# Batched 64x64 matmul: b in a block-diagonal tile by cast DMA, a loaded as fp32 in 2 KB runs and cast on VectorE

## The chip, the cores and the metric

The kernel runs on one core of a Trainium2 chip. The metric is the device time of one execution in microseconds; the time before is the median of three runs.

## The reference

```python
"a": np.random.randn(1024, 64, 64).astype(np.float32)
"b": np.random.randn(1024, 64, 64).astype(np.float32)

def reference(a, b):
    return np.matmul(a, b).astype(np.float32)
```

There are 1024 independent products of 64x64 matrices in fp32. Each of a, b and the output holds 4,194,304 numbers, 16.78 MB. Both kernels multiply in bf16 and accumulate in fp32.

## The kernel before

The 1024 matrices are worked off in 16 load groups of 64 (the loop over `lg`). A group has 32 pairs of matrices, and a pair stands on 128 partitions: the rows of the even matrix on partitions 0 to 63, those of the odd one on 64 to 127.

**Loads.** All loads are issued from GpSimd and cast fp32 to bf16 on the way. For a there are two loads a group (L70), one for each half of the partitions; they write only the two diagonal 64x64 blocks of `a_diag` (three buffers in turn, zeroed once by VectorE at L60). For b there are two loads a group (L77), each of 16 pairs. A row of a matrix is 64 numbers: 256 bytes in memory, 128 bytes as bf16.

**Compute.** A group is cut into four compute groups of 8 pairs (the loop over `cg`). TensorE transposes the 8 block-diagonal 128x128 blocks of a (L89), VectorE copies the result out of PSUM (L93), and then TensorE multiplies (L102). Each pair takes two matmuls, with 64 columns of the transposed a as weights, every second one, and the pair's b (64 columns) as the moving operand. The results go to PSUM partitions 0 to 63 or 64 to 127 by turns of two. VectorE copies one half of the results to `o_sb` (L112), ScalarE the other (L113).

**Stores.** Each group ends with one store of 1 MB from SyncE (L121): each partition reads 8 KB of `o_sb` and writes sixteen runs of 512 bytes. SyncE issues nothing else.

**Order.** Each engine works off its instructions in the order in which the tile framework's scheduler has placed them, and an instruction that waits holds up what stands behind it on its engine. Loads run ahead as far as there are buffers: three each of `a_diag`, `b_sb` and `o_sb`.

Of the kernel before, what the change touches and what calls it, by code (L numbers as in the profile page):

```python
# [1 line left out]

# [5 lines left out]

fp32 = mybir.dt.float32  # L10
bf16 = mybir.dt.bfloat16


@with_exitstack
def kernel(
    ctx: ExitStack,
    tc: tile.TileContext,
    a: bass.AP,
    b: bass.AP,
    out: bass.AP,  # L20
):
    nc = tc.nc

    B, M, K = a.shape
    _, _, N = b.shape
    assert (M, K, N) == (64, 64, 64)

    LG = 64 if B % 64 == 0 else B
    CG = 16
    STORE_BF16 = False  # L30
    A_BUFS = 3
    SBUF_BUFS = 3
    PSUM_BUFS = 3

    assert B % LG == 0 and LG % CG == 0
    n_lg = B // LG
    n_cg = LG // CG

    P2_LG = LG // 2
    P2_CG = CG // 2  # L40
    S4_CG = CG // 4

    a_v = a.rearrange("(g p h) r n -> g h r p n", p=P2_LG, h=2)
    b_v = b.rearrange("(g s h) r n -> g h r s n", s=P2_LG, h=2)

    consts = ctx.enter_context(tc.tile_pool(name="consts", bufs=1))
    a_pool = ctx.enter_context(tc.tile_pool(name="a_pool", bufs=1))
    lg_pool = ctx.enter_context(tc.tile_pool(name="lg", bufs=SBUF_BUFS))
    cg_pool = ctx.enter_context(tc.tile_pool(name="cg", bufs=2 * PSUM_BUFS))
    ps_pool = ctx.enter_context(  # L50
        tc.tile_pool(name="ps", bufs=PSUM_BUFS, space=bass.MemoryType.PSUM)
    )

    identity = consts.tile([128, 128], bf16)
    make_identity(nc, identity)

    a_tiles = []
    for ai in range(A_BUFS):
        a_diag = a_pool.tile([128, P2_LG, 128], bf16, name=f"a_diag_{ai}")
        nc.vector.memset(a_diag, 0.0)  # L60
        a_tiles.append(a_diag)

    out_dt = bf16 if STORE_BF16 else fp32

    for lg in range(n_lg):
        i0 = lg * LG

        a_sb = a_tiles[lg % A_BUFS]
        for h in range(2):
            nc.gpsimd.dma_start(  # L70
                out=a_sb[64 * h : 64 * h + 64, :, 64 * h : 64 * h + 64],
                in_=a_v[lg, h],
            )

        b_sb = lg_pool.tile([128, P2_LG, 64], bf16, name="b_sb")
        for s0 in range(0, P2_LG, P2_LG // 2):
            nc.gpsimd.dma_start(  # L77
                out=b_sb[:, s0 : s0 + P2_LG // 2, :],
                in_=b_v[lg, :, :, s0 : s0 + P2_LG // 2, :],
            )  # L80

        o_sb = lg_pool.tile([128, LG // 4, 128], out_dt, name="o_sb")

        for cg in range(n_cg):
            p0 = cg * P2_CG

            t_ps = ps_pool.tile([128, P2_CG, 128], bf16, name="t_ps")
            for pp in range(P2_CG):
                nc.tensor.transpose(  # L89
                    t_ps[:, pp, :], a_sb[:, p0 + pp, :], identity  # L90
                )
            t_sb = cg_pool.tile([128, P2_CG, 128], bf16, name="t_sb")
            nc.vector.tensor_copy(t_sb[:], t_ps[:])  # L93

            o_ps = ps_pool.tile([128, S4_CG, 128], fp32, name="o_ps")
            for pp in range(P2_CG):
                p = p0 + pp
                sigma, colp = pp // 2, pp % 2
                orows = slice(64 * colp, 64 * colp + 64)
                stat = t_sb[:, pp, :].rearrange("k (hh mm) -> k hh mm", hh=2)  # L100
                for j in range(2):
                    nc.tensor.matmul(  # L102
                        o_ps[orows, sigma, 64 * j : 64 * j + 64],
                        stat[:, :, j::2],
                        b_sb[:, p, :],
                        start=True,
                        stop=True,
                    )

            half = S4_CG // 2  # L110
            dst = o_sb[:, cg * S4_CG : (cg + 1) * S4_CG, :]
            nc.vector.tensor_copy(dst[:, :half, :], o_ps[:, :half, :])  # L112
            nc.scalar.copy(dst[:, half:, :], o_ps[:, half:, :])  # L113

        o_dst = out[i0 : i0 + LG].rearrange(
            "(q b4) (t u) c -> b4 t q u c", b4=4, u=2
        )
        if STORE_BF16:
            nc.gpsimd.dma_start(out=o_dst, in_=o_sb[:, :, :])
        else:  # L120
            nc.sync.dma_start(out=o_dst, in_=o_sb[:, :, :])  # L121


# [1 line left out]
_INS = ['a', 'b']  # L125
_OUTS = [((1024, 64, 64), 'float32')]


# [23 lines left out]
```

## Time and profile before

| what | value |
|---|---|
| device time, median of 3 runs | 188.72 us (188.5 to 189.0) |
| span of the profiled execution, first to last instruction | 186.4 us |
| difference, what lies around the span | 2.3 us |
| busy share of TensorE, VectorE, GpSimd, ScalarE | 48%, 40%, 39%, 13% |
| mean granted TensorE clock | 0.656 |
| moved by DMA, counted as it lands | 33.79 MB |
| read from and written to memory | 33.55 MB, 16.78 MB |

The profile shows one execution. A DMA row counts packets and the bytes that land: a load that casts counts its bf16 bytes, half of what it reads. The "share of 16 engines" adds up the times of packets, and packets of one engine can overlap, so it can pass 100%. PEclk and "granted clock" give the TensorE clock as a share of full speed. An engine name with a q (SPq, POOLq) is that engine's issuing queue.

### The profile page before, as it was taken

How to read it: one execution, taken by the hardware profiler on the slowest of the kernel's cores; microseconds unless marked ns; L12 is line 12 of the kernel's file. 1: busy time of each engine (PE TensorE's matmuls, PEld its weight loads, DVE VectorE, ACT ScalarE, POOL GpSimd, SP SyncE). 2: the span in 40 equal slices, each digit the busy share in tenths (PEclk: the TensorE clock that was granted, in tenths of full speed). 3: DMA queues.
4: the chain of work that ended last, by engine and by line, in shares of the span. 5: the costliest groups of instructions: out<-in, count | busy, mean ns of one | idle time of the engine just before them, and what ended most of it. 6: DMA issues, size and time to landing. Idle time of an engine off the chain costs nothing.

```text
span 186.4 us, 3567 instructions
## 1 busy us (share of the span) xinstructions
PE 90.0 (48%) x1536; PEld 75.9 (41%) x1536; DVE 74.6 (40%) x131; ACT 25.1 (13%) x65; POOL 72.4 (39%) x70
## 2 busy tenths in 40 slices
PE   0088126282444814629147480575704867174740
PEld 0077125271334713528036460464503756163630
DVE  6449323344134632426224270353602546044350
ACT  2011301102002110111101120021300113011020
POOL 7998422362424604255132642336322373200000
PEclk9999955559657685585855576555665556755585
DMA  5999999999999999999999999999999999999937
GB/s 36 143 156 157 186 212 213 165 169 215 183 208 157 182 206 186 201 158 194 194 196 192 158 201 186 206 182 157 215 177 212 171 158 204 183 212 177 236 103 205
DMA packets 165136, 33.79 MB, mean 181 GB/s; under 512 B 132352, under 2 KB 165120, under 8 KB 165120
## 3 DMA queue, kind: packets, MB, share of 16 engines
q0 software_dynamic: 132096, 16.78, 140.5%
q1 hardware_dynamic: 33024, 16.78, 42.4%
q8 instruction: 12, 0.20, 0.4%
q14 instruction: 4, 0.03, 0.0%
HBM read 33.55 MB, written 16.78 MB: 270 GB/s over the span
## 4 chain that ended last, share of the span: by engine, by line
DMA 69%; PE 13%; POOL 7%; issue 6%; DVE 2%; ACT 0%; POOLq 0%
DMA b_sb<-in_b_dram 58%; DMA a_diag<-in_a_dram 11%; PE t_ps L89 8%; PE o_ps L102 5%; POOL a_diag L70 4%; POOL b_sb L77 3%; DVE a_diag L60 1%; DVE t_sb L93 0%; DVE o_sb L112 0%; ACT o_sb L113 0%; POOLq L70 0%; POOLq L77 0%
## 5 line engine op out<-in xcount | busy, mean ns | idle before, releaser
L89 PE MATMUL t_ps<-identity,a_diag 128*128 128x128 bf16 x512 | 57.8, 293 | 61.2 <-DMA a_diag<-in_a_dram 61.2
L89 PEld LDWEIGHTS <-a_diag 128*128 128x128 bf16 x512 | 46.4, 134 | 64.4 <-issue 62.4
L93 DVE COPY t_sb<-t_ps 128x1024 bf16<-128x1024 bf16 x64 | 43.6, 691 | 70.6 <-PE t_ps L89 70.3
L77 POOL DMA_DIRECT2D b_sb<-in_b_dram x32 | 37.1, 1164 | 56.3 <-DMA a_diag<-in_a_dram 22.9
L102 PE MATMUL o_ps<-b_sb,t_sb 128*64 128x64 bf16 x1024 | 36.3, 230 | 28.3 <-DMA b_sb<-in_b_dram 24.9
L70 POOL DMA_DIRECT2D a_diag<-in_a_dram x32 | 34.9, 1093 | 31.8 <-DMA b_sb<-in_b_dram 22.5
L102 PEld LDWEIGHTS <-t_sb 128*64 128x64 bf16 x1024 | 29.5, 141 | 39.1 <-issue 19.4
L113 ACT COPY o_sb<-o_ps 128x256 f32<-128x256 f32 x64 | 23.8, 373 | 154.6 <-DVE o_sb L112 154.4
L112 DVE COPY o_sb<-o_ps 128x256 f32<-128x256 f32 x64 | 26.9, 424 | 32.8 <-PE o_ps L102 32.2
L60 DVE MEMSET a_diag<- 128x2048 uint32 x3 | 5.3, 1765 | 2.0 <-PEq L136 1.2
L113 ACT ACT_TABLE_LOAD x1 | 1.3, 1283 | 0.7 <-PEq L136 0.7
masks.py:199 POOL TENSOR_SCALAR_AFFINE_SELECT identity<-identity 128x128 bf16<-128x128 bf16 x1 | 0.3, 307 | 0.1
masks.py:197 POOL MEMSET identity<- 128x128 bf16 x1 | 0.2, 206 | 0.3 <-POOLq L136 0.3
L136 POOL MEMSET const-float32-0.0<- 128x1 f32 x1 | 0.1, 99 | 0.2 <-issue 0.2
L136 POOL MEMSET const-bfloat16-1.0<- 128x1 bf16 x1 | 0.1, 102 | 0.0
L136 POOL MEMSET const-uint8-127<- 128x1 uint8 x1 | 0.1, 102 | 0.0
L136 POOL MEMSET const-float32-1.0<- 128x1 f32 x1 | 0.1, 99 | 0.0
## 6 DMA issues: line engine op xcount, KB each, us to landing
out_dram<-o_sb SPq DMA_DIRECT2D x16, 1024.0 KB, 11.4
b_sb<-in_b_dram POOLq DMA_DIRECT2D x32, 256.0 KB, 19.1
a_diag<-in_a_dram POOLq DMA_DIRECT2D x32, 256.0 KB, 20.3
```

The lines of the kernel that those rows point to most:

```text
L60: nc.vector.memset(a_diag, 0.0)
L70: nc.gpsimd.dma_start(out=a_sb[64 * h : 64 * h + 64, :, 64 * h : 64 * h + 64], in_=a_v[lg, h],)
L77: nc.gpsimd.dma_start(out=b_sb[:, s0 : s0 + P2_LG // 2, :], in_=b_v[lg, :, :, s0 : s0 + P2_LG // 2, :],)
L89: nc.tensor.transpose(t_ps[:, pp, :], a_sb[:, p0 + pp, :], identity)
L93: nc.vector.tensor_copy(t_sb[:], t_ps[:])
L102: nc.tensor.matmul(o_ps[orows, sigma, 64 * j : 64 * j + 64], stat[:, :, j::2], b_sb[:, p, :], start=True, stop=True,)
L112: nc.vector.tensor_copy(dst[:, :half, :], o_ps[:, :half, :])
L113: nc.scalar.copy(dst[:, half:, :], o_ps[:, half:, :])
L136: nc = _bacc.Bacc("TRN2", target_bir_lowering=False, num_devices=1)
```

## The change

The work is still cut into 16 pieces (now called tiles, `t`) of 64 matrices, and the store is written in other words, with the same size and the same runs. The rest is new.

- **b** now makes the block diagonal. A tile of b is `b_bd`, 128 partitions by 16 by 4 by 128, with four buffers that VectorE zeroes at the start. Four matrices share a column of 128 partitions: matrix h stands on partitions 32h to 32h + 31, two rows side by side on each partition. So four loads a tile, each on 32 partitions, still cast from GpSimd, but with runs of 512 bytes in memory and 256 bytes in bf16.
- **a** is loaded as fp32 from SyncE, one load of 1 MB a tile, in runs of 2 KB, three tiles ahead, into four buffers. VectorE then casts it to bf16 and reorders it (`a_bf`).
- **TensorE** makes 16 transposes a tile (half as many as before), each of every second column of `a_bf`. VectorE copies them out of PSUM with a reordering read, four copies of 512 a tile. There are 64 matmuls a tile, as before, but each with 32 columns of weights, 256 columns of b (four blocks of 64) and an output on 32 PSUM partitions, the four strips of 32 in turn; two matmuls accumulate into each result.
- **Output copies** are one per 512 columns, two a tile on ScalarE and two on VectorE.

```diff
-        for h in range(2):
-            nc.gpsimd.dma_start(
-                out=a_sb[64 * h : 64 * h + 64, :, 64 * h : 64 * h + 64],
-                in_=a_v[lg, h],
-            )
...
-        for s0 in range(0, P2_LG, P2_LG // 2):
-            nc.gpsimd.dma_start(
-                out=b_sb[:, s0 : s0 + P2_LG // 2, :],
-                in_=b_v[lg, :, :, s0 : s0 + P2_LG // 2, :],
-            )
...
+    T = 64
+    n_t = B // T
+    AHEAD = 3
+    NB = 4
+    a_v = a.rearrange("(t h g) (mp v) k -> t (g mp) h (v k)", h=4, g=16, v=8)
+    b_v = b.rearrange("(t h g) (kp u) n -> t h kp g (u n)", h=4, g=16, u=2)
+    o_v = out.rearrange("(t hq g4) (mo w) n -> t (g4 mo) hq (w n)", hq=16, g4=4, w=2)
...
+    a_pool = ctx.enter_context(tc.tile_pool(name="a_pool", bufs=NB))
+    at_pool = ctx.enter_context(tc.tile_pool(name="at_pool", bufs=3))
+    o_pool = ctx.enter_context(tc.tile_pool(name="o_pool", bufs=3))
...
+    def load_a(t):
+        a_sb = a_pool.tile([128, 4, 8, 64], fp32, name="a_sb")
+        nc.sync.dma_start(
+            out=a_sb[:].rearrange("p h v k -> p h (v k)"), in_=a_v[t]
+        )
+        a_tiles[t] = a_sb
+    def load_b(t):
+        for h in range(4):
+            nc.gpsimd.dma_start(
+                out=b_tiles[t % NB][32 * h : 32 * h + 32, :, h, :], in_=b_v[t, h]
+            )
+    nc.vector.memset(b_tiles[0][:], 0.0)
+    load_a(0)
+    load_b(0)
+    identity = consts.tile([128, 128], bf16)
+    make_identity(nc, identity)
+    for i in range(1, NB):
+        nc.vector.memset(b_tiles[i][:], 0.0)
+    for t in range(1, AHEAD):
+        load_a(t)
+        load_b(t)
+    for t in range(n_t):
+        if t + AHEAD < n_t:
+            load_a(t + AHEAD)
+            load_b(t + AHEAD)
...
+        nc.vector.tensor_copy(
+            a_bf[:], a_sb[:].rearrange("p h v k -> p v h k")
+        )
+        a_cols = a_bf[:].rearrange("p v h k -> p v (h k)")
...
+                    nc.tensor.transpose(
+                        at_ps[:, vo, u, :], a_cols[:, 2 * vo + w, u::2], identity[:]
+                    )
...
+                nc.vector.tensor_copy(
+                    at_sb[:, w, u, :, :],
+                    at_ps[:, :, u, :].rearrange("p vo q -> p q vo"),
+                )
...
+        for gq in range(4):
+            o_ps = o_psum.tile([128, 2, 4, 64], fp32, name="o_ps")
+            for w in range(2):
+                for u in range(2):
+                    for g4 in range(4):
+                        g = 4 * gq + g4
+                        nc.tensor.matmul(
+                            o_ps[32 * g4 : 32 * g4 + 32, w, :, :],
+                            at_sb[:, w, u, 8 * g : 8 * g + 8, :].rearrange(
+                                "p mp vo -> p (mp vo)"
+                            ),
+                            b_bd[:, g, :, 64 * u : 64 * u + 64],
+                            start=(u == 0),
+                            stop=(u == 1),
+                        )
+            dst = o_sb[:, :, gq, :, :]
+            src = o_ps[:].rearrange("p w h n -> p h w n")
+            if gq % 2 == 0:
+                nc.scalar.copy(dst, src)
+            else:
+                nc.vector.tensor_copy(dst, src)
+        nc.sync.dma_start(
+            out=o_v[t], in_=o_sb[:].rearrange("p h q w n -> p (h q w n)")
+        )
```

More of the change, by code (lines that the diff above doesn't have):

```diff
@@ L25 @@
     _, _, N = b.shape
[L26 to L44, printed above, removed]
-    consts = ctx.enter_context(tc.tile_pool(name="consts", bufs=1))
@@ L47 @@
[L47 to L51, printed above, removed]
-    )
+    assert (M, K, N) == (64, 64, 64) and B % 64 == 0
+    T = 64
[3 more added lines that the diff above has]
+    a_v = a.rearrange("(t h g) (mp v) k -> t (g mp) h (v k)", h=4, g=16, v=8)
@@ new lines @@
+    b_v = b.rearrange("(t h g) (kp u) n -> t h kp g (u n)", h=4, g=16, u=2)
+    o_v = out.rearrange("(t hq g4) (mo w) n -> t (g4 mo) hq (w n)", hq=16, g4=4, w=2)
+    consts = ctx.enter_context(tc.tile_pool(name="consts", bufs=1))
+    a_pool = ctx.enter_context(tc.tile_pool(name="a_pool", bufs=NB))
+    at_pool = ctx.enter_context(tc.tile_pool(name="at_pool", bufs=3))
+    o_pool = ctx.enter_context(tc.tile_pool(name="o_pool", bufs=3))
+    t_psum = ctx.enter_context(
+        tc.tile_pool(name="t_psum", bufs=4, space=bass.MemoryType.PSUM)
+    )
@@ new lines @@
+    o_psum = ctx.enter_context(
+        tc.tile_pool(name="o_psum", bufs=4, space=bass.MemoryType.PSUM)
+    )
+    b_tiles = []
+    for i in range(NB):
+        b_bd = consts.tile([128, 16, 4, 128], bf16, name=f"b_bd{i}")
+        b_tiles.append(b_bd)
+    a_tiles = {}
+    def load_a(t):
[9 more added lines that the diff above has]
+            )
@@ L54 @@
+    nc.vector.memset(b_tiles[0][:], 0.0)
+    load_a(0)
+    load_b(0)
     identity = consts.tile([128, 128], bf16)
     make_identity(nc, identity)
[L57 to L68, printed above, removed]
-        for h in range(2):
-            nc.gpsimd.dma_start(
-                out=a_sb[64 * h : 64 * h + 64, :, 64 * h : 64 * h + 64],
-                in_=a_v[lg, h],
-            )
-        b_sb = lg_pool.tile([128, P2_LG, 64], bf16, name="b_sb")
-        for s0 in range(0, P2_LG, P2_LG // 2):
-            nc.gpsimd.dma_start(
-                out=b_sb[:, s0 : s0 + P2_LG // 2, :],
-                in_=b_v[lg, :, :, s0 : s0 + P2_LG // 2, :],
-            )
[L82 to L90, printed above, removed]
-                )
[L92 to L116, printed above, removed]
-        )
[L118 to L121, printed above, removed]
@@ new lines @@
+    for i in range(1, NB):
[7 more added lines that the diff above has]
+            load_b(t + AHEAD)
+        a_sb = a_tiles.pop(t)
+        b_bd = b_tiles[t % NB]
+        a_bf = at_pool.tile([128, 8, 4, 64], bf16, name="a_bf")
+        nc.vector.tensor_copy(
+            a_bf[:], a_sb[:].rearrange("p h v k -> p v h k")
+        )
+        a_cols = a_bf[:].rearrange("p v h k -> p v (h k)")
+        at_sb = at_pool.tile([128, 2, 2, 128, 4], bf16, name="at_sb")
+        for w in range(2):
+            at_ps = t_psum.tile([128, 4, 2, 128], bf16, name="at_ps")
+            for vo in range(4):
+                for u in range(2):
+                    nc.tensor.transpose(
+                        at_ps[:, vo, u, :], a_cols[:, 2 * vo + w, u::2], identity[:]
+                    )
+            for u in range(2):
+                nc.vector.tensor_copy(
+                    at_sb[:, w, u, :, :],
+                    at_ps[:, :, u, :].rearrange("p vo q -> p q vo"),
+                )
+        o_sb = o_pool.tile([128, 4, 4, 2, 64], fp32, name="o_sb")
+        for gq in range(4):
+            o_ps = o_psum.tile([128, 2, 4, 64], fp32, name="o_ps")
+            for w in range(2):
+                for u in range(2):
+                    for g4 in range(4):
[17 more added lines that the diff above has]
+            out=o_v[t], in_=o_sb[:].rearrange("p h q w n -> p (h q w n)")
+        )
```

## The prediction

> **What bounds the kernel now.** I read the page first: engines, DMA row, queues, chain.
>
> ```profile
> span 186.4 us, 3567 instructions
> PE 90.0 (48%) x1536; PEld 75.9 (41%) x1536; DVE 74.6 (40%) x131; ACT 25.1 (13%) x65; POOL 72.4 (39%) x70
> ...
> DMA  5999999999999999999999999999999999999937
> ...
> q0 software_dynamic: 132096, 16.78, 140.5%
> q1 hardware_dynamic: 33024, 16.78, 42.4%
> ...
> DMA b_sb<-in_b_dram 58%; DMA a_diag<-in_a_dram 11%; PE t_ps L89 8%; PE o_ps L102 5%; POOL a_diag L70 4%; POOL b_sb L77 3%; DVE a_diag L60 1%; DVE t_sb L93 0%; DVE o_sb L112 0%; ACT o_sb L113 0%; POOLq L70 0%; POOLq L77 0%
> ```
>
> No engine is busy half the span, the DMA engines nearly all of it, and 69% of the chain that ends last is loads. q0 holds the casting loads (some 131,072 packets of 128 bytes landing, 256 read), q1 the stores (32,768 of 512 bytes); the rest of their counts are small. So the price of a packet decides. The DMA view restricted to a stretch gives it. From 8 to 18 us only loads ran:
>
> ```profile
> q0 software_dynamic: 12301, 1.56, 244.8%
> ```
>
> From 23 to 28 us loads and stores ran side by side:
>
> ```profile
> q1 hardware_dynamic: 1675, 0.85, 83.1%
> q0 software_dynamic: 1671, 0.21, 64.3%
> ```
>
> From 181.5 to 185 us the last store ran alone:
>
> ```profile
> q1 hardware_dynamic: 1988, 1.01, 101.5%
> ```
>
> One of the 16 engines thus spends 10 us x 16 / 12,301 = **13.0 ns** on a load packet alone, 3.5 x 16 / 1,988 = **28.2 ns** on a store packet alone, and 5 x 16 / 1,673 = 47.8 ns on one of each (the two queues take turns one to one). A store beside a load thus costs 47.8 - 13.0 = **34.8 ns**.
>
> Does that add up to the span? Per engine there are 8,192 load packets and 2,048 store packets. The last store (128 packets an engine) runs alone, the other 1,920 pair with loads: 1,920 x 47.8 + 128 x 28.2 + 6,272 x 13.0 = 91.8 + 3.6 + 81.5 = 176.9 us. The windows view has the rest (after the engines, the granted clock, the DMA share and GB/s):
>
> ```profile
> 0.00:8.00 8.00, 0.00 (x0) 0.00 (x0) 5.29 (x3) 1.28 (x1) 6.68 (x12) 1.00 1.23 79
> 178.00:180.00 2.00, 1.12 (x36) 0.72 (x33) 1.82 (x4) 0.37 (x1) 0.00 (x0) 1.00 0.23 69
> 180.00:181.00 1.00, 0.00 (x0) 0.00 (x0) 0.00 (x0) 0.37 (x1) 0.00 (x0) 1.00 0.00 0
> 181.00:182.00 1.00, 0.00 (x0) 0.00 (x0) 0.00 (x0) 0.00 (x0) 0.00 (x0) 0.57 0.60 172
> 185.00:186.40 1.40, 0.00 (x0) 0.00 (x0) 0.00 (x0) 0.00 (x0) 0.00 (x0) 0.50 0.03 8
> ```
>
> The first 8 us moved 0.63 MB, 4.05 us at the 156 GB/s of the load stretch, so packets began at 3.95 us. Ahead of the last store the DMA engines stood for 1.5 + 1.0 + 0.4 = 2.9 us (the last group's compute), and 1.4 us follow it. 3.95 + 176.9 + 2.9 + 1.4 = 185.2 us; 1.2 of 186.4 stay unexplained. This sum I redo for the change.
>
> **The change: DMA.** Stores keep their 2,048 packets an engine: 1,920 x 34.8 + 128 x 28.2 = **70.4 us** (57.8 were all as cheap as alone; 81.3 at the 39.7 ns for which a mixed store packet was busy, 83.1% of 5 us x 16 / 1,675).
>
> Loads fall from 8,192 packets to 2,048 of b (512 bytes read) and 512 of a (2 KB). Neither size was loaded before. If a packet costs what the 256-byte one costs whatever its size, b takes 2,048 x 13.0 = 26.6 us; if price goes with bytes, 26.0 ns and 53.2 us; at the store's 28.2 ns, 57.8 us. For a the ends are 28.2 ns (a 512-byte packet, however long) and 4 x 28.2 = 112.8 ns: 14.4 and 57.8 us; by bytes from the load row it is 104 ns, 53.2 us. The rows speak for bytes more than for packets (19.7 bytes a ns in the load, 18.2 in the store), yet a store writes memory and may be dear for that. I take a price three quarters of the way from packets to bytes: 22.8 ns for b, **46.7 us**, and 81.3 ns for a, **41.6 us**. That three quarters is my choice and the softest number here. The loads fall from 106.5 to 88.3 us, the DMA work from 176.9 to 158.7 us.
>
> The Trainium skill (DMA: Bandwidth & Descriptors, "Why small descriptors are slow") puts a fixed 3 cycles on each packet beside one per 32 bytes: 11 cycles for 256 bytes, 19 for 512. Scaled to the measured 13.0 ns this estimate is 22.5 ns for b and 79.2 ns for a, a DMA sum of 157.0 us, where the rows by bytes give 176.8. By the same rule a 512-byte store would take 22.5 ns; the lone store's 28.2 ns does not agree.
>
> **The start and SyncE.** Before, SyncE issues only stores:
>
> ```order
> L121 DMA out_0_dram<-o_sb_467 128x16x128 [waits Activation_49]
> L121 DMA out_0_dram<-o_sb_594 128x16x128 [waits Activation_49]
> L121 DMA out_0_dram<-o_sb_721 128x16x128 [waits Activation_49]
> L121 DMA out_0_dram<-o_sb_848 128x16x128 [waits Activation_49]
> L121 DMA out_0_dram<-o_sb_975 128x16x128 [waits Activation_49]
> ```
>
> Now a's loads stand between them; here those of tiles 8 to 13 around the stores of tiles 3 and 4 (`o_sb_450`, `o_sb_555`):
>
> ```order
> L59 DMA a_sb_629<-in_a_dram 128x4x512 [waits DMAHW4_49]
> L59 DMA a_sb_734<-in_a_dram 128x4x512 [waits DMAHW5_49]
> L59 DMA a_sb_839<-in_a_dram 128x4x512 [waits DMAHW6_49,DVE_49]
> L130 DMA out_0_dram<-o_sb_450 128x16x128 [waits DVE_49,Activation_49]
> L59 DMA a_sb_944<-in_a_dram 128x4x512 [waits DMAHW7_49,DMAHW1_49]
> L59 DMA a_sb_1049<-in_a_dram 128x4x512 [waits DMAHW3_49,DMAHW0_49]
> L59 DMA a_sb_1154<-in_a_dram 128x4x512 [waits DMAHW4_49,DVE_49]
> L130 DMA out_0_dram<-o_sb_555 128x16x128 [waits DMAHW2_49,DVE_49,Activation_49]
> ```
>
> Tile 4's store now stands behind the load of tile 13, which waits for VectorE to free tile 9's buffer. While SyncE waits there, loads issued before it and those of b still flow.
>
> The first four loads of a wait for nothing. From issue to first packet I take 1.0 us, from the last store, issued at 180.43 us, with packets from 181.4:
>
> ```profile
> 180.43 0.37 SPq L121 DMA_DIRECT2D out_dram<-o_sb  x1
> ...
> SPq L136 <- PEq L136: 0.7, 1, 0.7
> ```
>
> SyncE is free after 0.7 us, so packets begin near 1.8 us. VectorE first zeroes four tiles of 4,096 words, twice the size of before's three: 4 x (3.53 + 0.38 of pause) = 15.6 us, so the first cast ends near 19 us. Until then the DMA engines have a for four tiles (128 packets an engine x 81.3 = 10.4 us) and b for three (8.7): busy until 20.9. At the cheap ends of both prices this cover is 3.6 + 5.0 us, and up to 9 us would stand empty.
>
> **VectorE.** The groups with their mean times:
>
> ```profile
> L93 DVE COPY t_sb<-t_ps 128x1024 bf16<-128x1024 bf16 x64 | 43.6, 691 | 70.6 <-PE t_ps L89 70.3
> L77 POOL DMA_DIRECT2D b_sb<-in_b_dram x32 | 37.1, 1164 | 56.3 <-DMA a_diag<-in_a_dram 22.9
> L113 ACT COPY o_sb<-o_ps 128x256 f32<-128x256 f32 x64 | 23.8, 373 | 154.6 <-DVE o_sb L112 154.4
> L112 DVE COPY o_sb<-o_ps 128x256 f32<-128x256 f32 x64 | 26.9, 424 | 32.8 <-PE o_ps L102 32.2
> L60 DVE MEMSET a_diag<- 128x2048 uint32 x3 | 5.3, 1765 | 2.0 <-PEq L136 1.2
> ```
>
> Zeroing: 4 x 3.53 = 14.1 us. Sixteen casts of 2,048: between 2 x 691 and 8 x 424 ns; I take 1.9 us, near the memset of as many words: 30.4. Sixty-four reordering copies of 512: between half of 691 and 2 x 424 ns; I take 0.6 us: 38.4. Thirty-two output copies of 512: 0.75 us (at most 848 ns): 24.0. Together 107 us, at the upper ends 150: both under 158.7. Its order mixes the stages. Before, copies of transposes and of outputs alternate:
>
> ```order
> L93 COPY t_sb_350<-t_ps_341 128x1024 [waits DVE_49,PE_49]
> L93 COPY t_sb_380<-t_ps_371 128x1024 [waits DVE_49,PE_49]
> L112 COPY o_sb_340<-o_ps_352 128x256 [waits PE_49]
> L112 COPY o_sb_340<-o_ps_382 128x256 [waits PE_49]
> L93 COPY t_sb_410<-t_ps_401 128x1024 [waits DVE_49,PE_49]
> ```
>
> Now three casts (tiles 9, 10, 11) stand between the outputs of tiles 3 and 4:
>
> ```order
> L128 COPY o_sb_450<-o_ps_505 128x4x128 [waits PE_49]
> L102 COPY at_sb_742<-at_ps_743 128x512 [waits DVE_49,PE_49]
> L102 COPY at_sb_742<-at_ps_743 128x512
> L102 COPY at_sb_742<-at_ps_754 128x512 [waits PE_49]
> L102 COPY at_sb_742<-at_ps_754 128x512
> L88 CAST a_bf_1055<-a_sb_734 128x2048 [waits DMAHW4_49,DVE_49]
> L88 CAST a_bf_1160<-a_sb_839 128x2048 [waits DMAHW5_49,DVE_49,PE_49]
> L88 CAST a_bf_1265<-a_sb_944 128x2048 [waits DMAHW7_49,DVE_49,PE_49]
> L128 COPY o_sb_555<-o_ps_574 128x4x128 [waits DMAHW0_49,PE_49,Activation_49]
> ```
>
> Tile 4's outputs now wait for tile 11's a to land. Loads are only drawn ahead of stores by this; the work for the DMA engines stays the same, so I count nothing.
>
> **TensorE, GpSimd, ScalarE.** From the chain and the timeline (the last row at granted clock 1.00, the first two at 0.50, as the two window rows say):
>
> ```profile
> 54.86 0.57 PE o_ps L102 x16
> 55.44 1.62 PE t_ps L89 x14
> ...
> 15.79 1.62 PE L89 MATMUL t_ps<-identity,a_diag 128*128 128x128 bf16 x25
> ...
> 13.00:18.00 5.00, 4.52 (x110) 3.86 (x107) 4.07 (x8) 1.39 (x4) 4.75 (x5) 1.00 2.45 156
> 53.90:57.10 3.20, 3.14 (x48) 2.55 (x48) 1.56 (x4) 0.75 (x2) 1.08 (x1) 0.50 1.94 185
> ```
>
> At 0.50 a transpose of 128 columns takes 116 ns (0.90 ns a column), a matmul of 64 columns 36 ns (0.56): matmuls to the two halves of PSUM's partitions overlap in part. With 256 columns at 0.56 a matmul takes 143 ns; with four strips in turn I halve that to 72. 1,024 x 72 + 256 x 116 = 73 + 30 = 103 us even at 0.50, hidden. GpSimd still issues 64 loads, at most 64 x 1.16 = 74 us; ScalarE takes at most 32 x 0.75 = 24 us. Both are hidden.
>
> **Sum.** 1.8 + 158.7 + 2.9 + 1.4 + 1.2 = 166.0 us of span, 20.4 less than before. The 2.9 us of idle at the end I keep: it is nothing if queued stores cover the last tile, up to 9.2 us (64 matmuls at 143 ns) if not. Around the profiled span lie 188.7 - 186.4 = 2.3 us to the median, so I forecast **168.3 us**.
>
> **Rivals.**
>
> *Bytes, not packets.* A load costs by its bytes, or a's 2 KB runs go out in small packets. Loads then stay at 106.4 us, 18.1 more: 186.4 us. For it: the like bytes per ns of the two rows. Against: a packet that has no fixed part at all would be odd with 2.4 of them in flight at once. Chance 0.15.
>
> *The order leaves holes.* SyncE's stores behind loads that wait for casts, and VectorE's outputs behind casts that wait for loads, let the DMA queues run dry. If each of 16 tiles costs one bare issue of 1.0 us, it is 168.3 + 16 = 184.3 us. For it: the two chains shown. Against: b's loads, up to four tiles ahead, do not hang on SyncE. Chance 0.15.
>
> *TensorE becomes the bound* (slower). Four strips overlap no better than two and the clock stays at 0.50: 1,024 x 143 + 29.7 = 176 us from the first transpose near 19 us, then 0.7 of copy, a store of 4.6 and 1.4: 202 us of span, 204 in all. A matmul over some 127 ns makes it slower than before ((186.4 - 19 - 8 - 29.7) / 1,024). Against: TensorE at work 90% of the time had the clock at 1.00 (13 to 18 us), and there even 256 columns without overlap take 130 ns. Chance 0.08. The Trainium skill (TensorE: Matmul & The Clock Gate, "Part 3: Packing small matmuls") lets a weight load overlap matmuls in flight only when their row groups differ; all matmuls here use all 128 rows, so by that rule nothing would overlap, 0.90 x 256 = 232 ns each at 0.50, about 295 us. The 36 ns, less than the 58 that 64 columns take at 0.90, do not agree with it.
>
> **How the numbers follow.** The forecast's case has 0.60; 0.02 is left for what I have not thought of. The range runs down to 151: both load prices halfway between packets and bytes (19.5 and 58.5 ns) take 18.4 us off, less 1 for the start. Up to 187 it takes in the byte case and the holes. A measurement can tell about 0.3% from no change, 0.6 us. Faster: 0.60, plus 0.07 of the byte case (which ends 1.2% under before, with its unknowns on both sides) and 0.14 of the holes: 0.81. Same: 0.04 and 0.01: 0.05. Slower: 0.04 of the byte case, 0.08 of TensorE, 0.02 of the rest: 0.14.
>
> **What would show it.** In the profile after: packets near 8,192 of 2 KB and 65,536 more in all; in a stretch of loads alone, over 312 GB/s read; DMA share near full from 2 us on; VectorE under 130 us; a matmul well under 127 ns. It is wrong if a 2 KB packet takes 100 ns or more, if DMA slices stand under half in the middle, or if TensorE or VectorE is busy most of the span.

## The result, and the profile after

| | before | after |
|---|---|---|
| device time, median | 188.86 us (188.5 to 189.34) | 166.96 us (165.06 to 167.58) |
| span of the profiled execution | 186.4 us | 164.9 us |
| ratio after to before | | 0.880 (0.875 to 0.886) |

The forecast was 168.3 us, 151 to 187. The page of the changed kernel, the lines that answer to those of before:

```profile
span 164.9 us, 2995 instructions
PE 71.9 (44%) x1280; PEld 54.9 (33%) x1280; DVE 92.3 (56%) x116; ACT 19.3 (12%) x33; POOL 44.7 (27%) x70
...
DMA  5999999999999999999999999999999999999995
...
q1 hardware_dynamic: 41472, 33.56, 74.6%
q0 software_dynamic: 33792, 8.39, 50.4%
...
DMA out_dram<-o_sb 21%; DMA a_sb<-in_a_dram 20%; PE o_ps L114 16%; DVE at_sb L102 11%; DVE b_bd L76 6%; PE at_ps L98 4%; DVE o_sb L128 3%; DVE a_bf L88 2%; DVE b_bd L70 2%; ACT o_sb L126 1%; SPq L130 1%; ACTq L126 0%; DVEq L88 0%; DVEq L102 0%; SPq L59 0%
```

The DMA row is still full from end to end; only what fills it is cheaper. q1 now holds 32,768 store packets and 8,192 of a, q0 32,768 packets of b (the rest of their counts are packets of 4 bytes). The chain names VectorE and TensorE more often than before, but a chain through full queues tells little: the DMA row is the one to read.

The prices come from five stretches of the DMA view. Loads of a alone, 3 to 9 us (1,094 packets of 2 KB among the 1,126):

```profile
q1 hardware_dynamic: 1126, 2.24, 101.5%
```

Loads of b alone, 16 to 19.5 us:

```profile
q0 software_dynamic: 2515, 0.62, 181.2%
```

Stores (q1) beside loads of b, 112 to 142 us:

```profile
q1 hardware_dynamic: 8416, 4.27, 69.4%
q0 software_dynamic: 8432, 2.09, 68.6%
```

Stores alone, 156.5 to 162 us:

```profile
q1 hardware_dynamic: 3113, 1.59, 102.2%
```

Loads of a (q1) beside loads of b, 26 to 30 us:

```profile
q1 hardware_dynamic: 566, 1.13, 83.5%
q0 software_dynamic: 564, 0.14, 34.5%
```

With 16 engines that is 6 x 16 / 1,094 = 87.7 ns for 2 KB of a, 22.3 ns for 512 bytes of b, 28.3 ns for a store alone, 57.0 ns for a store and a b packet (so 34.7 ns for the mixed store), 113.3 ns for an a and a b packet (3.3 more than the two alone).

Two of the lone prices move with the stretch. From 4 to 8 us the first row below holds 776 packets of a and 24 of 4 bytes, 82.5 ns a packet. The second is from 148 to 154 us of the kernel with four loads of a (first experiment): 3,939 stores alone and 29 packets of 4 bytes, 24.4 ns a store. No run shows what sets the difference.

```profile
q1 hardware_dynamic: 800, 1.59, 103.9%
```

```profile
q1 hardware_dynamic: 3968, 2.02, 112.5%
```

By these prices the excess of a pair over the two alone is 3.3 to 8.5 ns for a with b, and 6.4 to 10.3 ns for a store with b.

From 148.3 to 163.0 us almost only stores run, at 28.3 ns some 520 packets an engine. So b is 2,048 x 22.3 = 45.7 us, a 512 x 87.7 = 44.9, stores 1,528 x 34.7 + 520 x 28.3 = 67.7: 158.3 us, 18.6 less than the 176.9 of before. This takes every store ahead of 148.3 us as mixed. Counted over the whole trace, microsecond by microsecond, only some 1,310 stores of an engine start beside a packet of b, and so do some 350 packets of a; with these counts the sum is 45.7 + 44.9 + 350 x 3.3 + 1,310 x 34.7 + 738 x 28.3 = 158.1 us. The total stands, to the 3 us or so by which the lone prices move. The first packets come at 1.85 us but flow without a pause only from 2.5 us, and 1.9 us follow the last one; 2.2 us of the span are left over.

### The profile page after: what moved, and what is told of

Same layout as the page of the kernel before. It is cut to its first block, busy times and chain, and to the rows that moved or that the text cites. A ratio compares the mean times of both kernels' runs of the same rounds, so it can differ in the third digit from the quotient of the medians.

```text
span 164.9 us, 2995 instructions
## 1 busy us (share of the span) xinstructions
PE 71.9 (44%) x1280; PEld 54.9 (33%) x1280; DVE 92.3 (56%) x116; ACT 19.3 (12%) x33; POOL 44.7 (27%) x70
## 4 chain that ended last, share of the span: by engine, by line
DMA 41%; DVE 25%; PE 21%; issue 6%; ACT 1%; SPq 1%; DVEq 0%; ACTq 0%
DMA out_dram<-o_sb 21%; DMA a_sb<-in_a_dram 20%; PE o_ps L114 16%; DVE at_sb L102 11%; DVE b_bd L76 6%; PE at_ps L98 4%; DVE o_sb L128 3%; DVE a_bf L88 2%; DVE b_bd L70 2%; ACT o_sb L126 1%; SPq L130 1%; ACTq L126 0%; DVEq L88 0%; DVEq L102 0%; SPq L59 0%
## 5 line engine op out<-in xcount | busy, mean ns | idle before, releaser
L66 POOL DMA_DIRECT2D b_bd<-in_b_dram x64 | 44.0, 692 | 90.9 <-PE o_ps L114 62.7
L98 PE MATMUL at_ps<-identity,a_bf 128*128 128x128 bf16 x256 | 26.0, 268 | 70.2 <-DVE at_sb L102 41.2
L114 PE MATMUL o_ps<-b_bd,at_sb 128*32 128x256 bf16 x1024 | 47.3, 358 | 13.6 <-ACT o_sb L126 11.8
L98 PEld LDWEIGHTS <-a_bf 128*128 128x128 bf16 x256 | 20.8, 121 | 75.2 <-DVE a_bf L88 29.6
L114 PEld LDWEIGHTS <-at_sb 128*32 128x32 bf16 x1024 | 34.1, 126 | 25.1 <-issue 14.3
L102 DVE COPY at_sb<-at_ps 128x512 bf16<-128x512 bf16 x64 | 39.4, 678 | 0.0
L88 DVE CAST a_bf<-a_sb 128x2048 bf16<-128x2048 f32 x16 | 19.5, 1236 | 31.9 <-DMA a_sb<-in_a_dram 27.4
L128 DVE COPY o_sb<-o_ps 128x512 f32<-128x512 f32 x32 | 21.4, 688 | 28.2 <-PE o_ps L114 14.5
L126 ACT COPY o_sb<-o_ps 128x512 f32<-128x512 f32 x32 | 18.1, 587 | 135.5 <-PE o_ps L114 107.9
L76 DVE MEMSET b_bd<- 128x4096 uint32 x3 | 10.4, 3472 | 2.4 <-issue 2.4
L70 DVE MEMSET b_bd<- 128x4096 uint32 x1 | 3.5, 3472 | 1.7 <-PEq L147 1.7
## 6 DMA issues: line engine op xcount, KB each, us to landing
b_bd<-in_b_dram POOLq DMA_DIRECT2D x64, 128.0 KB, 13.1
```

The costliest lines, as they stand in the source:

```text
L66: nc.gpsimd.dma_start(out=b_tiles[t % NB][32 * h : 32 * h + 32, :, h, :], in_=b_v[t, h])
L70: nc.vector.memset(b_tiles[0][:], 0.0)
L76: nc.vector.memset(b_tiles[i][:], 0.0)
L88: nc.vector.tensor_copy(a_bf[:], a_sb[:].rearrange("p h v k -> p v h k"))
L98: nc.tensor.transpose(at_ps[:, vo, u, :], a_cols[:, 2 * vo + w, u::2], identity[:])
L102: nc.vector.tensor_copy(at_sb[:, w, u, :, :], at_ps[:, :, u, :].rearrange("p vo q -> p q vo"),)
```

## The experiments

The theory under test: the DMA engines are the bound; a packet costs a small fixed part plus its bytes, so fewer, longer load packets made the gain. Rivals: a load costs by its bytes, and a gained only by leaving the casting GpSimd queue; or the order on SyncE and GpSimd sets the time. Two questions came from the profile after: what makes a mixed store dearer than a lone one, and whether strips of output partitions overlap on TensorE, on which the price of the matmuls hung. All ratios below are to the kernel before.

### Four loads for one, runs kept

```diff
-        nc.sync.dma_start(
-            out=a_sb[:].rearrange("p h v k -> p h (v k)"), in_=a_v[t]
-        )
+        for h in range(4):
+            nc.sync.dma_start(
+                out=a_sb[:, h].rearrange("p v k -> p (v k)"), in_=a_v[t, :, h]
+            )
```

> Control: each 1 MB load of a is issued as four loads of 256 KB, the runs stay 2 KB. Theory (a load packet costs a small fixed part plus its bytes, the DMA engines are the bound, the number of issues is hidden): within 2 us of the changed kernel's 167.0 us. Rival (the order of loads and stores on SyncE sets the time): 64 loads of a in place of 16 shift the order and the time moves by over 3 us.

Measured: 165.5 us, ratio 0.879 (0.876 to 0.882), 1.5 us under the changed kernel. The number of issues on SyncE does not cost, and another order of its loads and stores moves the time by less than 1%.

### a in runs of 256 bytes

```diff
-            nc.sync.dma_start(
-                out=a_sb[:, h].rearrange("p v k -> p (v k)"), in_=a_v[t, :, h]
-            )
+            nc.sync.dma_start(out=a_sb[:, :, h, :], in_=a_v[t, h])
```

`a_sb` is laid out as `[128, 8, 4, 64]` here, and `a_v` by t, h, partition, v, k.

> a comes in runs of 256 bytes (65,536 packets, still fp32 from SyncE, four loads a tile, already in the order of the cast), b and stores as in the changed kernel. Theory (fixed part plus bytes): 4,096 packets per DMA engine at 13.0 ns in place of 512 at 87.7 ns is 53.2 in place of 44.9 us, so 8 us over the control with 2 KB runs, about 175 us. Rival (a costs by its bytes, the gain came from taking a off the casting GpSimd queue): no change against the control, about 167 us.

Measured: 194.5 us, ratio 1.030 (1.025 to 1.036): 29.0 us over its control, slower than the kernel before. The direction is the theory's, the size three and a half times as large. Its DMA view shows why; from 3 to 8 us a ran practically alone:

```profile
q1 hardware_dynamic: 4579, 1.15, 128.9%
q0 software_dynamic: 41, 0.01, 2.1%
```

and from 25 to 29 us beside b:

```profile
q0 software_dynamic: 1365, 0.34, 83.5%
q1 hardware_dynamic: 1345, 0.34, 64.2%
```

A plain 256-byte packet takes 5 x 16 / 4,579 = 17.5 ns (15.7 from 3 to 5 us, 18.5 from 5 to 7), not the 13.0 ns of before's casting one, of which half as much lands. 4,096 x 17.5 = 71.7 us against 44.9 is 26.8 of the 29 us. From 17.5 ns at 256 bytes and 87.7 at 2 KB the price has a fixed part of 7.5 ns and 10.0 per 256 bytes; with the spread of both prices the fixed part lies between 5.4 and 9.4 ns. The second stretch shows something else: a pair takes 4 x 16 / 1,355 = 47.2 ns, the two alone 17.5 + 22.3 = 39.8. Here both are loads, and still 7.4 ns come on top (6.4 to 9.2 by the spread) when two queues take turns.

### b in eight loads, and in runs of 256 bytes

The control, then the kernel with short runs (where `b_bd` is laid out as `[128, 16, 2, 4, 64]`, `b_v` and the matmuls to match):

```diff
-            nc.gpsimd.dma_start(
-                out=b_tiles[t % NB][32 * h : 32 * h + 32, :, h, :], in_=b_v[t, h]
-            )
+            for g0 in (0, 8):
+                nc.gpsimd.dma_start(
+                    out=b_tiles[t % NB][32 * h : 32 * h + 32, g0 : g0 + 8, h, :],
+                    in_=b_v[t, h, :, g0 : g0 + 8, :],
+                )
...
+            for u in range(2):
+                nc.gpsimd.dma_start(
+                    out=b_tiles[t % NB][32 * h : 32 * h + 32, :, u, h, :],
+                    in_=b_v[t, h, u],
+                )
```

> Control: each load of b is issued as two, of 8 groups each, runs of 512 bytes kept. Theory: 128 issues on GpSimd at 0.69 us or less are 88 us, hidden beside the DMA engines: within 2 us of 167.0 us. Rival (GpSimd's issues or its order are on the path): over 3 us slower.

> b comes in runs of 256 bytes read and 128 landing (65,536 packets, as in the kernel before), eight loads a tile, a and stores as in the changed kernel. Theory (fixed part plus bytes): 4,096 packets per DMA engine at 13.0 ns in place of 2,048 at 22.3 ns is 53.2 in place of 45.7 us: 7.5 us over the control with 512-byte runs, about 175 us. Rival (cost goes with bytes): no change against the control.

Measured: the control 169.9 us, ratio 0.902 (0.899 to 0.906); the short runs 177.4 us (173.9 to 179.7; these executions spread too much for a ratio). The control is 3 us slower than the changed kernel, more than expected, and the waits view says on what:

```profile
POOL b_bd L67 <- DMA b_bd<-in_b_dram: 51.7, 71, 3.1
```

In the changed kernel the same row reads:

```profile
POOL b_bd L66 <- DMA b_bd<-in_b_dram: 21.7, 17, 2.9
```

GpSimd waited 51.7 us in all (71 times, 3.1 us at most) for its own earlier loads, against 21.7: with half as much in each load, fewer bytes are under way, and b's queue runs dry. From 16 to 20 us, with b alone, the control's DMA row falls to 0; the changed kernel's has only nines from 16 to 19.5 us:

```profile
DMA  9999999999999999974338999999999731210018
```

The short runs then cost 7.5 us more in the medians, just what the packet prices give, but with that spread and a control that is itself disturbed this pair supports the theory rather than proves it. The firmer proof for b is the price of its packets: 22.3 ns for 512 bytes, where two of 256 took 26.0 in the kernel before. In the kernel with short runs b ran alone from 16 to 17 us, and a packet of 256 bytes took 1 x 16 / 1,217 = 13.1 ns there too:

```profile
q0 software_dynamic: 1217, 0.15, 238.7%
```

### The order of the strips on TensorE

First the four matmuls of a strip of 32 output partitions in a row (the loop over `g4` made the outer one of a group), then all 16 of a tile (outside the loop over `gq` too, with four `o_ps` open):

```diff
-            for w in range(2):
-                for u in range(2):
-                    for g4 in range(4):
+            for g4 in range(4):
+                for w in range(2):
+                    for u in range(2):
```

> The loop over the four strips of 32 output partitions is made the outer one: the four matmuls of a strip follow each other, and the strips no longer take turns. Nothing else changes. Theory (strips in turn overlap; a strip alone does not): a matmul of 256 columns then takes 130 ns (granted clock 1.00) to 232 ns (0.50) in place of the 43 ns of the changed kernel (64 in 2.75 us), 8.3 to 14.8 us a tile with 1.9 of transposes; at the upper end TensorE becomes the bound and the time is 180 to 270 us, at the lower end it stays hidden, 167 to 172. Rival (256 columns are simply fast, whatever the strip): 43 ns a matmul and 167 us.

> Like the kernel with runs of four, but all 16 matmuls of a tile that go to one strip of 32 output partitions follow each other, then the next strip's. Theory (strips overlap, and the short runs of four were bridged by matmuls of the next strip): the 64 matmuls of a tile now take clearly longer than 2.75 us, 6.9 us at 107 ns a matmul or more; TensorE stays under the DMA engines' 10 us a tile, so 167 to 175 us. Rival (256 columns of 32 weight columns are fast whatever the strip): still 2.7 to 3.6 us a tile.

Measured: 166.9 us, ratio 0.877 (0.868 to 0.885), and 184.8 us, ratio 0.976 (0.970 to 0.982). The 64 matmuls of one tile on the timeline, in the changed kernel, with runs of four, with runs of 16:

```profile
122.17 2.72 PE L114 MATMUL o_ps<-b_bd,at_sb 128*32 128x256 bf16 x64
```

```profile
123.37 2.70 PE L114 MATMUL o_ps<-b_bd,at_sb 128*32 128x256 bf16 x64
```

```profile
137.38 5.90 PE L117 MATMUL o_ps<-b_bd,at_sb 128*32 128x256 bf16 x64
```

The windows view of the first and the third of these stretches has the granted clock (the third number from the end), 0.70 and 1.00; with runs of four it was 0.72:

```profile
122.17:124.90 2.73, 2.72 (x65) 2.05 (x65) 0.69 (x1) 0.97 (x2) 0.00 (x0) 0.70 1.39 214
```

```profile
137.38:143.30 5.92, 5.90 (x66) 5.17 (x65) 0.69 (x1) 1.00 (x2) 0.00 (x0) 1.00 1.19 197
```

With runs of four nothing changes, so the theory's first form, that strips must take turns one by one, falls. With runs of 16 a matmul takes 92 ns in place of 43, although the clock was higher. So strips do overlap, the overlap bridges a run of four, and most of it is lost over a run of 16; how TensorE does it no run shows. The time rose more than the theory said (184.8 against 167 to 175). GpSimd now waited longer for the matmuls ahead of b's loads, 93.2 us against 62.7 in the changed kernel:

```profile
POOL b_bd L66 <- PE o_ps L117: 93.2, 11, 20.3
```

The matmuls of three tiles in a row start at 126.89, 137.38 and 147.39 us, over 10 us apart, no less than the 158.3 / 16 = 9.9 us that the DMA engines need for a tile. The edit also makes all four `o_ps` of a tile finish together, and what that adds to the dearer matmul was not tried apart. The DMA row of this kernel has gaps in its second half, which the changed kernel's has not:

```profile
DMA  4999999999999999999999895998949695999666
```

As far as this run tells, it takes the overlap of the strips to keep TensorE hidden in the changed kernel.

### Where the stores are issued

```diff
-        nc.sync.dma_start(
+        nc.gpsimd.dma_start(
             out=o_v[t], in_=o_sb[:].rearrange("p h q w n -> p (h q w n)")
         )
```

The second kernel has `nc.scalar.dma_start` there; the third has GpSimd for the loads of a as well; the fourth GpSimd for a, with the stores left on SyncE.

> Stores are issued from GpSimd, in one queue with the loads of b; a alone stays on SyncE. Theory (two queues that take turns on an engine cost 6.4 ns for each pair of a store and a b packet): some 1,580 pairs an engine disappear, up to 10 us less, 157 to 162 us, and in stretches of stores and b alone a pair takes 50.6 in place of 57.0 ns. Rival (reads and writes of the memory hinder each other, whatever the queue): a pair still takes 57 ns and the time stays at 167 us. Rival (order): loads of b now stand behind stores that wait for compute; holes open and the time rises over 170 us.

> Stores are issued from ScalarE, so loads of a and stores no longer stand in one line on SyncE. Theory (the DMA engines are full, the order on SyncE hides nothing): within 3 us of 167 us. Rival (SyncE's line leaves holes): over 4 us faster. If turns between queues cost time, a third queue that takes turns would rather make it slower.

> All loads and stores are issued from GpSimd, one queue for everything. Theory (turns between queues cost): no pair is left, 45.7 for b, 44.9 for a and 58.0 for stores (28.3 ns each) are 148.6 us of DMA work, with 4 us of start and end about 153 us of span, 155 us, if the one line leaves no holes. Rival (reads against writes): about 167 us. Rival (order): the first a stands behind VectorE's zeroing and loads behind waiting stores; slower than 170 us.

> Only the loads of a move to GpSimd, in one queue with b; stores alone stay on SyncE in packets of 512 bytes. Theory (turns between two queues cost, and so do short store packets; both hang on the stores): stores still take turns with loads, nearly all 2,048 packets an engine at 34.7 ns, so 45.7 + 45 + 70 = 161 us of DMA work and 4 of start and end, 165 us of span, 167 us. Rival (whatever goes through GpSimd is quicker): 157 us or less. Rival (one line on GpSimd leaves holes): over 172 us.

| kernel | us | ratio to before |
|---|---|---|
| stores on GpSimd | 148.8 | 0.787 (0.782 to 0.793) |
| stores on ScalarE | 165.9 | 0.877 (0.870 to 0.883) |
| a and stores on GpSimd | 158.4 (155.0 to 162.9) | spread too wide |
| a alone on GpSimd | 166.6 | 0.882 (0.877 to 0.886) |

Stores on GpSimd beat both kernels. The page of that kernel, and its DMA view from 134 to 137 us, stores alone, and from 100 to 110, stores and b:

```profile
span 147.1 us, 2999 instructions
...
q0 software_dynamic: 38144, 25.17, 90.0%
q1 hardware_dynamic: 8448, 16.78, 33.1%
...
HBM read 33.55 MB, written 16.78 MB: 342 GB/s over the span
```

```profile
DMA  7997999999796949699999999959958989999939
q0 software_dynamic: 244, 0.95, 101.8%
```

```profile
DMA packets 3434, 2.75 MB, mean 275 GB/s; under 512 B 2942, under 2 KB 2942, under 8 KB 3433
```

Two things changed. A store from GpSimd goes out in packets of 4 KB, eight runs each: q0 has 38,144 packets, where 32,768 short ones would have been added to its 33,792. Alone, 232 such packets (12 of the 244 have 4 bytes) take 3 x 16 / 232 = 206.9 ns each, 25.9 for a run, with the engines not quite full, as the row shows. Single runs from SyncE took 24.4 to 28.3 ns alone, so that the longer packet is cheaper is not shown. And beside b nothing comes on top: of the 160 us of engine time from 100 to 110 us, 491 of these packets take 101.6, which leaves 58.4 us for 2,942 packets of b, 19.9 ns each, no more than alone. With b at its 22.3 ns it is the stores that come out cheaper, 192 ns a packet and 24.0 a run.

Stores thus cost 2,048 x 25.9 = 53.0 us or 2,048 x 24.0 = 49.2, which is 14.7 to 18.5 less than the 67.7 before; the span fell by 17.8 us. How much of this is turns saved and how much longer packets, no run separates: with lone stores from SyncE at 28.3 ns the turns are 9.7 us of it (67.7 less 2,048 x 28.3), with 24.4 they are 17.7.

That reads and writes of the memory hinder each other as such is made unlikely by the 7.4 ns between two kinds of loads above. It is not refuted: in GpSimd's one queue, loads and stores went out largely one after the other. From 105 to 106 us, for one, there were packets of b alone:

```profile
DMA packets 685, 0.17 MB, mean 170 GB/s; under 512 B 685, under 2 KB 685, under 8 KB 685
```

That SyncE's line leaves holes falls with the stores on ScalarE: the time moved by 1.1 us, and a store and a b packet still take 56.9 ns (110 to 140 us). That GpSimd's path is quicker for anything falls with a alone on GpSimd: no gain, as forecast. With all on GpSimd the time fell too, to 3 us over its forecast of 155, but the executions lie up to 8 us apart; why it is not as good as stores alone on GpSimd stays open. Part of it may be the end, where its DMA engines were busy only 45% of 145 to 150 us.

## Why the prediction was right

**The sum.** The mechanism was right: full DMA engines, and fewer, longer load packets to fill them. DMA work was put at 158.7 us and measures 158.3, but that the two agree so closely is luck. The terms erred apart and cancel: a 41.6 against 44.9 us, b 46.7 against 45.7, stores 70.4 against 67.7. For b, "three quarters of the way from packets to bytes" was a choice without a row behind it, and held: 22.8 ns against 22.3. For a the same choice gave 81.3 ns, against 87.7 from 3 to 9 us and 82.5 from 4 to 8. It scaled the price of a casting packet, of which half the bytes land, and at 256 bytes a plain one is dearer, 17.5 against 13.0 ns; at 2 KB no casting packet was measured. The rule of the Trainium skill (DMA: Bandwidth & Descriptors, "Why small descriptors are slow") gave, as an estimate, 22.5 and 79.2 ns: right for b, further off than mine for a.

**Mixed stores** kept their price, 34.7 against 34.8 ns. They were cheaper in sum because more of them ran without a load beside them, by the count above some 738 an engine and not 128. What the prediction took as a property of stores beside loads shows between two kinds of loads as well, and not within GpSimd's one queue; that reading was not in it.

**The ends.** The first packets came at 1.85 us (1.8 forecast), and they flow without a pause from 2.5 us. The 2.9 us of idle ahead of the last store are gone but for a dip near 151 us, since queued stores covered the last tile, as the prediction allowed without counting it. Against that, 2.2 us of the span stay unexplained, where 1.2 were put down. The last packets and the end of the span:

```profile
160.00:163.00 3.00, 0.00 (x0) 0.00 (x0) 0.00 (x0) 0.00 (x0) 0.00 (x0) 0.50 1.02 292
164.00:164.90 0.90, 0.00 (x0) 0.00 (x0) 0.00 (x0) 0.00 (x0) 0.00 (x0) 0.50 0.00 0
```

**What was to be hidden was hidden.** The groups of the changed kernel:

```profile
L66 POOL DMA_DIRECT2D b_bd<-in_b_dram x64 | 44.0, 692 | 90.9 <-PE o_ps L114 62.7
L114 PE MATMUL o_ps<-b_bd,at_sb 128*32 128x256 bf16 x1024 | 47.3, 358 | 13.6 <-ACT o_sb L126 11.8
L102 DVE COPY at_sb<-at_ps 128x512 bf16<-128x512 bf16 x64 | 39.4, 678 | 0.0
L88 DVE CAST a_bf<-a_sb 128x2048 bf16<-128x2048 f32 x16 | 19.5, 1236 | 31.9 <-DMA a_sb<-in_a_dram 27.4
L128 DVE COPY o_sb<-o_ps 128x512 f32<-128x512 f32 x32 | 21.4, 688 | 28.2 <-PE o_ps L114 14.5
```

VectorE's 107 us were 92.3: the casts took 1.24 us, not 1.9, the reordering copies 0.68, not 0.6. TensorE's matmuls took 43 ns at a granted clock of 0.70, not 72 at 0.50; at 0.50 it would be some 60 ns, an estimate from these two figures.

**The rivals.** Bytes, not packets: refuted by a in runs of 256 bytes, 29 us over its control with the same bytes, and by b's prices. Holes from the order: SyncE did wait, 58.5 us for output copies by the waits view,

```profile
SPq L130 <- DVE o_sb L128: 58.5, 15, 9.5
```

but the DMA row shows no hole, and taking stores out of its line brought 1.1 us. TensorE as the bound: its deciding point was 127 ns a matmul; it took 43, and 92 in runs of 16, where the strips overlapped less. The rule of the Trainium skill that a weight load overlaps matmuls only across row groups (TensorE: Matmul & The Clock Gate, "Part 3: Packing small matmuls") does not agree with 43 ns for a load and a matmul that both use all rows: four of them take 172 ns at a granted clock of 0.70, no more than the 130 / 0.70 = 186 ns that the prediction's 130 ns at 1.00 would make of one alone.

## What to carry to other kernels

Where the DMA row is full, price the packet, not the byte: take stretches in which one kind runs alone, and one in which two run together, and make the span out of the counts. A lone price is the mean of its stretch, so take it from two before building on a few nanoseconds. A price holds for its kind; casting and plain loads of the same run differ. When two queues are busy at once, the pair's excess over the two alone is worth a term of its own, and putting both kinds into one queue is worth a trial.

## What the runs showed of the hardware

- Packets of two queues that take turns on a DMA engine cost more a pair than the two alone, whether both load or one stores: 6.4 to 9.2 ns for 256 bytes of a with b, 3.3 to 8.5 for 2 KB of a with b, 6.4 to 10.3 for a store with b. The ranges come from lone prices that differ by stretch.
- Stores of 512-byte runs issued from GpSimd went out eight runs to a packet and took 24.0 to 25.9 ns a run. From SyncE each run was a packet, of 24.4 to 28.3 ns alone and 34.7 beside b.
- A plain load packet of 256 bytes took 15.7 to 18.5 ns, a casting one that reads as much 13.0.
- Matmuls to different strips of 32 output partitions overlapped: 43 ns each in turn (granted clock 0.70) or in runs of four (0.72), 92 ns in runs of 16 (1.00).
